# The output product of a hybrid decoder block as seven block products, with x loaded into the collecting tile

## The chip, the cores and the metric

The kernel runs on one core of a Trainium2 chip. The metric is device time in microseconds. A core has TensorE (PE, with its weight loads shown as PEld), VectorE (DVE), ScalarE (ACT), GpSimd (POOL) and SyncE (SP); each works through its own instructions in a fixed order. SP, ACT and POOL also issue DMAs, each through a queue of its own; DMAs that add into their target are issued by POOL in this kernel. On PE the clock that was granted is given in the profile as a share of full speed.

## The reference

One layer of a decoder trunk on 512 tokens with a width of 1024, all in float32. Three mixers (sparse attention, block-sparse attention, a state-space scan) are projected to the width, gated and added; the sum goes through W_out, and then comes a feed-forward block of width 4096:

```python
mix = (gates[:, :, 0] * (y_a @ w_br_dsa[l]) + gates[:, :, 1] * (y_b @ w_br_nsa[l])
       + gates[:, :, 2] * (y_c @ w_br_ssd[l]))
x = x + mix @ w_out[l]
h = rms_norm(x, norm2_g[l])
x = x + jnp.square(jax.nn.relu(h @ w_ff1[l])) @ w_ff2[l]
```

The change concerns the line with `w_out` and the norm behind it.

## The kernel before, in words

**Products.** Both operands of a large product are split into a high part (rounded by a copy to fp32r) and a low part (the rest). `mm3` issues three matmuls into the same accumulator: high × high (L454), low × high (L455), high × low (L456). All work is in this form, so a weight block costs a copy on ACT (`whi`, L173) and a subtraction on DVE or POOL (`wlo`, L175).

**The weight stream.** A class `WS` holds all weight blocks of 128 x 1024 in their order of use. `load` starts the DMA of a block on SP into one of three raw buffers (`wraw`, RAWB = 3); `split` makes the high and low parts (six pairs); a raw buffer is free again when its low part is made. `tick` keeps the splits up to three blocks ahead of use and the loads up to three ahead of the splits.

**The end of the mixers.** The generator `branches` goes through six branches; the last, b2, adds the last 256 tokens of the block-sparse mixer to `mix` (128 partitions x 8 blocks of channels x 512 tokens, held transposed). Its matmuls are 256 columns wide. For every block of channels the finished sum is split into `mixh` and `mixl` with the factor 0.5 (L1608, L1609). Then W_out follows in two halves of 512 columns: for each of four blocks of 128 tokens 8 x 3 matmuls (192 in all, 128x512). DVE adds x from its own tile `xin` (L1631) into the collecting tile `x2`; ACT squares with a sum (L1633); two small steps on DVE (L1635, L1636) and a power on POOL (L1637) give the factor of the norm; DVE writes the normed tokens `xn` (L1641); PE transposes them in eight 128x128 steps (L1647); ACT and DVE split them into `h2h` and `h2l` (L1649, L1650). x and the gain g2b come over ACT's queue, W_out's blocks over SP's.

**The feed-forward block.** `F q m` names block m of the first FF product in quarter q. The first four blocks of quarter 0 are done in two token halves of 256, so that the first half needs token blocks 0 and 1 alone. The second FF product is already done with seven block products instead of eight, quarter by quarter: `quad_block` makes the weight sums, three of them in place in the two tiles qd0 and qd1 by accumulating DMAs on POOL's queue (L275), one (t3) by an accumulating DMA onto a raw tile (L260); `left` makes the quarters of the left operand and splits them (L1727, L1728); `ff_down` issues 24 matmuls per product and adds the result to `x2` and a spare accumulator `U2`. In the last quarter these sums are made by POOL (`sums`, `less`, L1691).

**What sets the order.** The program text is written by generators that take turns (`yield` gives the length of a piece); a scheduler then sets each engine's order by its own model of the times, with priorities (`high_priority`) that pull pieces forward. The order does not change at run time.

## Time and profile before

| | us |
|---|---|
| median of three timed runs (1345.57 to 1347.51) | 1347.01 |
| the profiled execution | 1348.56 |
| its span, first to last instruction | 1346.8 |
| first matmul of W_out, from the span's start | 962.87 |
| first matmul of the feed-forward block | 1010.04 |

The mean granted clock of TensorE is 0.997. Times of instructions below are counted from the start of the span. A row of a timeline gives start, duration, engine, line, operation, result and operands, and in square brackets how long the engine had stood idle and what ended it. In a row of grouped lines the last parts are busy time and mean ns. "L1631" is line 1631 of the kernel before.

### The profile page before, as it was taken

The numbers are of one execution on the slowest core, as the hardware profiler recorded it, in microseconds if no ns is written. First come the engines' busy times: TensorE is split into PE (matmuls) and PEld (weight loads), VectorE is DVE, ScalarE is ACT, GpSimd is POOL, SyncE is SP. The second block draws the span as 40 slices with busy tenths as digits, with TensorE's granted clock in tenths as the row PEclk, the third lists the DMA queues.
The fourth block names the chain that finished last, engine by engine and source line by source line (L and its number), as shares of the span: only waits on it lengthen the run. The fifth ranks groups of instructions, "written<-read, shape, count | busy, mean of one in ns | idle before, by whom it ended". The sixth has DMA issues, their size and how long they took to land.

```text
span 1346.8 us, 19610 instructions
## 1 busy us (share of the span) xinstructions
PE 1325.0 (98%) x6803; PEld 1102.9 (82%) x6803; DVE 1011.8 (75%) x1994; ACT 739.4 (55%) x1408; POOL 301.3 (22%) x258
## 2 busy tenths in 40 slices
PE   9999999999999998999999999999999999999998
PEld 7888888888877876888888888778889888888886
DVE  6499986989967656576687889979655566667767
ACT  5455335687767766366676566655333443444452
POOL 2225111111016666600000022224000100201154
PEclk9999999999999999999999999999999999999999
DMA  6436665454579899644354546335526474756554
GB/s 200 122 91 169 186 180 135 133 153 131 145 232 326 268 290 295 183 145 118 105 155 132 156 130 181 110 98 166 187 64 188 117 179 125 172 151 156 162 110 125
DMA packets 253953, 217.94 MB, mean 162 GB/s; under 512 B 16009, under 2 KB 203293, under 8 KB 253854
## 3 DMA queue, kind: packets, MB, share of 16 engines
q1 hardware_dynamic: 209916, 164.76, 41.0%
q0 software_dynamic: 17408, 25.17, 10.1%
q10 hardware_dynamic: 26530, 26.75, 6.0%
q8 instruction: 54, 0.88, 0.3%
q14 instruction: 45, 0.37, 0.1%
...
## 4 chain that ended last, share of the span: by engine, by line
PE 80%; DMA 6%; DVE 5%; POOL 4%; issue 3%; ACT 1%; SPq 0%; POOLq 0%; ACTq 0%; DVEq 0%
PE pj L454 19%; PE pj L456 18%; PE pj L455 18%; PE sc L454 3%; PE sc L455 3%; PE sc L456 3%; PE pT L983 3%; PE pv L996 2%; PE pv L995 2%; PE sc L924 2%; PE sc L923 2%; DMA wraw<-in_w_in_dram 1%; DMA xs<-x_d 1%; DVE wlo L175 1%; DMA xz<-xzt_d 1%
## 5 line engine op out<-in xcount | busy, mean ns | idle before, releaser
L173 ACT ACTIVATE whi<-wraw 128x1024 fp32r<-128x1024 f32 (+2 forms) x188 | 196.3, 1047 | 235.6 <-PE pj L455 130.5
L175 DVE TENSOR_TENSOR wlo<-wraw,whi 128x1024 fp32r<-128x1024 f32 (+1 forms) x176 | 221.4, 1261 | 105.5 <-ACT whi L173 102.6
L454 PE MATMUL pj<-hTh,whi 128*128 128x512 f32 x512 | 204.3, 399 | 2.2 <-DVE cacc L851 2.2
L456 PE MATMUL pj<-hTh,wlo 128*128 128x512 f32 x512 | 203.0, 397 | 0.0
L455 PE MATMUL pj<-hTl,whi 128*128 128x512 f32 x512 | 202.9, 396 | 0.0
L932 ACT ACTIVATE p<-p,nb,rs 128x384 f32<-128x384 f32 (+3 forms) x160 | 107.8, 677 | 25.9 <-DVE nb L930 25.8
L454 PEld LDWEIGHTS pj<-hTh,whi 128*128 128x128 f32 x512 | 96.6, 189 | 21.3 <-ACT eab L1340 2.2
L456 PEld LDWEIGHTS pj<-hTh,wlo 128*128 128x128 f32 x512 | 96.7, 189 | 19.7 <-issue 0.8
L455 PEld LDWEIGHTS pj<-hTl,whi 128*128 128x128 f32 x512 | 96.7, 189 | 18.7 <-issue 0.6
L455 PE MATMUL pj<-h2l,whi 128*128 128x512 f32 (+1 forms) x256 | 96.3, 376 | 0.0
L456 PE MATMUL pj<-h2h,wlo 128*128 128x512 f32 (+1 forms) x256 | 96.2, 376 | 0.0
L454 PE MATMUL pj<-h2h,whi 128*128 128x512 f32 (+1 forms) x256 | 96.1, 376 | 0.0
L1042 POOL DMA_DIRECT2D qu<-q_d x32 | 23.6, 738 | 269.5 <-PE sc L924 102.3
L454 PE MATMUL pj<-whi,hTh 128*128 128x512 f32 (+2 forms) x208 | 80.5, 387 | 0.4 <-DVE cacc L851 0.4
L456 PE MATMUL pj<-whi,hTl 128*128 128x512 f32 (+2 forms) x208 | 80.3, 386 | 0.1
L455 PE MATMUL pj<-wlo,hTh 128*128 128x512 f32 (+2 forms) x208 | 79.4, 382 | 0.0
L456 PE MATMUL sc<-whi,fo 128*128 128x512 f32 x200 | 77.7, 390 | 1.7 <-DVE fo L1728 1.7
L454 PE MATMUL sc<-whi,fh 128*128 128x512 f32 x200 | 77.8, 389 | 0.0
L455 PE MATMUL sc<-wlo,fh 128*128 128x512 f32 x200 | 77.8, 389 | 0.0
L987 ACT ACTIVATE pth<-pT 128x512 fp32r<-128x512 f32 x92 | 53.0, 594 | 31.6 <-PE pT L983 31.0
L1606 POOL TENSOR_TENSOR mixf<-mixf,gld 128x512 f32<-128x512 f32 x22 | 39.4, 1796 | 118.8 <-DVE gld L1605 97.7
L988 DVE TENSOR_TENSOR ptl<-pT,pth 128x512 fp32r<-128x512 f32 x92 | 61.6, 679 | 4.7 <-ACT pth L987 4.6
...
## 6 DMA issues: line engine op xcount, KB each, us to landing
wraw<-in_w_in_dram SPq DMA_DIRECT2D x84, 512.0 KB, 4.1
wraw<-in_w_ff_dram SPq DMA_DIRECT2D x56, 512.0 KB, 4.2
qd<-in_w_ff_dram POOLq DMA_DIRECT2D x24, 512.0 KB, 5.9
...
E<-ac_d SPq DMA_DIRECT2D x16, 512.0 KB, 5.8
xz<-xzt_d SPq DMA_DIRECT2D x16, 512.0 KB, 4.8
wraw<-in_w_br_ssd_dram SPq DMA_DIRECT2D x16, 512.0 KB, 4.5
```

Of the source, the lines that this page charges most:

```text
L173: act.activation(hi[:, :m], r[:, :m], AF.Copy)
L175: (pool if i in LOWP else dve).tensor_tensor(lo[:, :m], r[:, :m], f(hi[:, :m]), op=ALU.subtract)
L454: pe.matmul(o, lh, rh, start=first, stop=False)
L455: pe.matmul(o, lh, rl, start=False, stop=False)
L456: pe.matmul(o, ll, rh, start=False, stop=last)
L923: pe.matmul(s_[:, h % w, :n], u.q[h], kh[:, :n], start=True, stop=False)
L924: pe.matmul(s_[:, h % w, :n], u.q[h], kl[:, :n], start=False, stop=True)
L932: act.activation(u.p[h][:, :n], u.p[h][:, :n], AF.Exp, bias=u.nb[:, h:h + 1], scale=rs8[:, u.b, u.h0 + h:u.h0 + h + 1], accum_out=u.sm[:, ...
L983: pe.transpose(pt[:, h], u.p[h][:, kb * 128:kb * 128 + 128], ident)
L987: act.activation(ph, ptf, AF.Copy)
L988: dve.tensor_tensor(pl, ptf, f(ph), op=ALU.subtract)
L1606: (dve if br in ("b1", "b2") else pool).tensor_tensor(mx, mx, th, op=ALU.add)
```

## The change

W_out is taken out of the stream as eight blocks of two column halves, and put in as a further "quarter" q = -1 of the seven-product scheme, in the order P0, P6, P1, P2, P4, P3, P5 (the numbers are those of `PROD`; 24 matmuls each). The left operand is quartered from `mix` itself, with the difference tiles made by POOL and DVE; the high parts are copies on ACT (L1524), the low parts DVE's, and POOL's for P0 and P6 (L1525). The factor 0.5 moves into the evacuations: L1569 on DVE, or L1557 and L1565 on ACT followed by an add on POOL (L1561, L1566). x is loaded straight into `x2` at the start of b2. W_out's quarters 11 go to qd0 and qd1, which exist only from the moment when the attention's pool is closed and b2's begins; the sums follow by accumulating DMAs (now L280, and L265 onto a raw tile). The norm's small steps are all on POOL (L1763 to L1765). Tokens 0 to 255 are finished with P4, tokens 256 to 511 with P3 and P5, so squares and norm of each half are issued there. Four low parts of weights go to POOL (`LOWW`): one of t2, and FF blocks 1 to 3.

```diff
@@ -172,7 +172,7 @@
             with tc.issue_after(HX[HB[i]][0]) if i in HB else nullcontext():
                 act.activation(hi[:, :m], r[:, :m], AF.Copy)
             with tc.issue_after(H0[0][1]) if i == 1 else nullcontext():
-                (pool if i in LOWP else dve).tensor_tensor(lo[:, :m], r[:, :m], f(hi[:, :m]), op=ALU.subtract)
+                (pool if i in LOWP or i in LOWW else dve).tensor_tensor(lo[:, :m], r[:, :m], f(hi[:, :m]), op=ALU.subtract)
...
         def tick(s):
             while s.nsplit < len(s.specs) and s.nsplit < min(s.consumed - 1 + NS, s.cur + LEAD):
+                if s.nload <= s.nsplit and s.shut():
+                    break
                 s.split()
             while s.nload < len(s.specs) and s.nload < s.nsplit + RAWB:
-                if callable(s.specs[s.nload][0]) and FL[0] is None:
+                if s.shut():
                     break
                 s.load()
+
+        def shut(s):
+            go = s.specs[s.nload][0]
+            return callable(go) and (FL[0] is None or (go.q >= 0) != FL[1])
...
-    P["wo"] = [plan_tok(A["w_out"], D, [(o * 512, 512)]) for o in range(2)]
...
-            return wcols(A["w_ff2"], D, 8 * q + 4 * row + 2 * s, 2, 512 * col, 512)
+            return wcols(A["w_out"] if q < 0 else A["w_ff2"], D, 8 * max(q, 0) + 4 * row + 2 * s, 2, 512 * col, 512)
...
                 if name == "11":
-                    t = FL[0].tile([128, 1024], F32, name=f"qd{s}", bufs=QB)
+                    t = FL[0].tile([128, 1024], F32, name=f"qd{s}", bufs=1 if q < 0 else QB)
                     nc.sync.dma_start(t.rearrange("p (a b) -> p a b", b=512), src("11"))
...
-    FL = [None]
-    FSEQ = [("F", 0, m) for m in range(8)]
+    FL = [None, False]
+    LOWW = set()
+    PLO = (0, 6)
+    FSEQ = [("G", -1, i) for i in (0, 6, 1, 2, 4, 3, 5)] + [("F", 0, m) for m in range(8)]
...
             ff[kind, q, i] = plan_ch(A["w_ff1"], 4096, q * 1024 + 128 * i)
+            if q == 0 and i in (1,2,3):
+                LOWW.add(ff[kind, q, i])
         else:
             ff[kind, q, i] = [quad_block(q, i, s) for s in range(2)]
+            if q < 0 and i in (2,):
+                LOWW.add(ff[kind, q, i][1])
...
+        ST, AO, FA, PRE = {}, {}, {}, {}
+
+        def quarters(q):
+            if q < 0:
+                return [mix[:, 4 * kh:4 * kh + 4, 256 * th:256 * th + 256] for kh, th in ((0, 0), (0, 1), (1, 0), (1, 1))]
+            return [FA[q, kh][:, th] if (q, kh) in FA else None for kh, th in ((0, 0), (0, 1), (1, 0), (1, 1))]
+
+        def less(name, a, b, eng=pool):
+            t = PRE.pop(name, None)
+            if t is None:
+                t = FL[0].tile([128, 4, 256], F32, name=name)
+            eng.tensor_tensor(t, a, b, op=ALU.subtract)
+            return t
+
+        def sums(q, part=None):
+            a11, a21, a12, a22 = quarters(q)
+            if part != 1:
+                if q < 0:
+                    ST[3] = less("fs3", a11, a21)
+                    return
+            ST[1] = less("fs", a21, a22, dve if q < 0 else pool)
+            ST[2] = less("fs2", a11, ST[1])
+            if q >= 0:
+                ST[3] = less("fs3", a11, a21)
+            ST[4] = less("fs4", a12, ST[2])
+
+        def left(n):
+            if n >= len(GSEQ):
+                return
+            q, i = GSEQ[n]
...
+            src = a11 if i == 0 else a22 if i == 5 else a12 if i == 6 else ST[i]
+            h_ = FL[0].tile([128, 4, 256], F32R, name="fh", bufs=2)
+            l_ = FL[0].tile([128, 4, 256], F32R, name="fo", bufs=2)
+            act.activation(h_, src, AF.Copy)
+            (pool if q < 0 and i in PLO else dve).tensor_tensor(l_, src, f(h_), op=ALU.subtract)
+            AO[q, i] = h_, l_
...
+        INTO = (((X11, PL), (UU, PL)), ((X22, PL), (X12, PL)), ((UU, MI),), ((X22, MI), (X21, PL)), ((X12, PL),), ((X21, PL),),
+                ((X11, PL),))
...
+        def ff_down(q, i):
+            ah, al = AO.pop((q, i))
+            pos = GSEQ.index((q, i))
+            blk = [ws.get(b) for b in ff["G", q, i]]
+            for tt in range(2):
+                p = ps(("pT", "sc", "pj")[pos and 2 - pos % 2] if q < 0 else "sc" if pos % 2 or q < 3 else "pT", [128, 512])
+                for j in range(4):
+                    wh, wl = blk[j // 2]
+                    cs = slice(128 * tt, 128 * tt + 128)
+                    mm3(p, ah[:, j, cs], al[:, j, cs], wh[:, j % 2], wl[:, j % 2], j == 0, j == 3)
+                    if tt and j % 2:
+                        ws.free(ff["G", q, i][j // 2])
+                    if tt == 0 and j == 1:
+                        left(pos + 1)
+                    yield 3 * 213
+                into = list(INTO[i])
+                if q in (-1, 0, 3) and i == 0:
+                    act.activation(UU(tt), p, AF.Copy, scale=0.5 if q < 0 else 1.0)
+                    into.pop()
+                    if q != 0:
+                        into.pop()
+                        pool.tensor_tensor(X11(tt), X11(tt), UU(tt), op=ALU.add)
+                if q in (-1, 3) and i == 1:
+                    into.pop()
+                    t1 = FL[0].tile([128, 512], F32, name="t1", bufs=2)
+                    act.activation(t1, p, AF.Copy, scale=0.5 if q < 0 else 1.0)
+                    pool.tensor_tensor(X12(tt), X12(tt), t1, op=ALU.add)
+                for d, op in into:
+                    if q < 0:
+                        dve.scalar_tensor_tensor(d(tt), p, 0.5 if op is PL else -0.5, d(tt), op0=ALU.mult, op1=ALU.add)
+                    else:
+                        dve.tensor_tensor(d(tt), d(tt), p, op=op)
+                if i == 2 and q in (-1, 2, 3):
+                    for d, op in ((X12, MI), (X21, PL), (X22, MI)):
+                        with tc.high_priority(offset=600 if q < 0 and d is X12 else 0):
+                            (dve if q == 2 or q < 0 and d is X12 else pool).tensor_tensor(d(tt), d(tt), UU(tt), op=op)
+                if q < 0:
+                    run_later()
+                    with tc.high_priority(offset=600):
+                        if i == 6:
+                            square(tt, 0)
+                        elif i == 4:
+                            square(tt, 1)
+                            norm(tt)
+                        elif i == 3:
+                            square(2 + tt, 1)
+                        elif i == 5:
+                            square(2 + tt, 0)
+                            norm(2 + tt)
...
-                mp = popen("mix", side="right")
-                mixh = mp.tile([128, KT, S], F32R, name="mixh")
-                mixl = mp.tile([128, KT, S], F32R, name="mixl")
+                fp = popen("ff", side="right")
+                wl = FL[0] = popen("wol", side="right")
+                U2 = wl.tile([128, 2, 512], F32, name="u2acc")
+                x2 = fp.tile([128, NB, D], F32, name="x2")
+                for t in range(NB):
+                    act.dma_start(x2[:, t], dram(A["x"], t * 128 * D, [[D, 128], [1, D]]))
+                left(0)
+                left(1)
+                for n in ("fs", "fs2", "fs3", "fs4"):
+                    PRE[n] = wl.tile([128, 4, 256], F32, name=n)
+                ws.tick()
...
-                if br == "b2":
-                    act.activation(mixh[:, m], mix[:, m], AF.Copy, scale=0.5)
-                    dve.scalar_tensor_tensor(mixl[:, m], mix[:, m], 0.5, f(mixh[:, m]), op0=ALU.mult, op1=ALU.subtract)
+                if br == "b2" and m in (3, 7):
+                    sums(-1, m // 7)
...
+        def square(t, o):
+            jk = n2.tile([128, 512], F32, name="jk2", bufs=1)
+            act.activation(jk, x2[:, t, o * 512:o * 512 + 512], AF.Square, accum_out=st2[:, t, o:o + 1])
+
+        def norm(t):
+            pool.tensor_tensor(st2[:, t, 2:3], st2[:, t, 0:1], st2[:, t, 1:2], op=ALU.add)
+            pool.tensor_scalar(st2[:, t, 2:3], st2[:, t, 2:3], 1.0 / D, EPS, op0=ALU.mult, op1=ALU.add)
+            pool.tensor_tensor(st2[:, t, 3:4], st2[:, t, 2:3], mhalf[:, :1], op=ALU.pow)
+            xn = n2.tile([128, D], F32, name="xn2", bufs=2)
+            for k0 in range(0, KT, 4):
+                cs = slice(k0 * 128, k0 * 128 + 512)
+                dve.scalar_tensor_tensor(xn[:, cs], x2[:, t, cs], st2[:, t, 3:4], g2b[:, cs], op0=ALU.mult, op1=ALU.mult)
+
+            def tr():
+                for k0 in range(0, KT, 4):
+                    p_ = ps("pT", [128, 4, 128])
+                    for k in range(4):
+                        pe.transpose(p_[:, k], xn[:, (k0 + k) * 128:(k0 + k + 1) * 128], ident)
+                    hsl = (slice(None), slice(k0, k0 + 4), slice(t * 128, t * 128 + 128))
+                    act.activation(h2h[hsl], p_, AF.Copy)
+                    dve.tensor_tensor(h2l[hsl], p_, f(h2h[hsl]), op=ALU.subtract)
+            defer(0, tr)
+
+        for q, i in GSEQ:
+            if q < 0:
+                yield from ff_down(q, i)
...
+        pclose("wol")
+        pclose("br")
+        pclose("gt")
         XT[0] = None
         fl = FL[0] = popen("ffl")
+        FL[1] = True
```

Three places show how the orders move. Lines of the changed kernel have other numbers: mm3 is L465 to L467, the transposes L1775, h2h and h2l L1777 and L1778, xn L1769.

POOL before, from the last add of the mixers to the FF stage (`st2` is the norm's factor, four times):

```order
L1606 TENSOR_TENSOR mixf_7601<-mixf_7601,gld_9666 128x512
L1606 TENSOR_TENSOR mixf_7601<-mixf_7601,gld_9713 128x512
L1637 TENSOR_TENSOR st2_10433<-st2_10433,mhalf_164 128x1 x4
L275 DMA qd0_10938<-in_w_ff2_dram 128x2x512
L275 DMA qd1_11027<-in_w_ff2_dram 128x2x512
```

POOL now, behind the first product (P0): `u2acc` holds P0, `fs2` to `fs4` are quarters of the left operand, `qd` and `wraw` weight sums:

```order
L1561 TENSOR_TENSOR x2_10285<-x2_10285,u2acc_10284 128x512
L1484 TENSOR_TENSOR fs3_10300<-mixf_7601 128x1024
L1561 TENSOR_TENSOR x2_10285<-x2_10285,u2acc_10284 128x512
L280 DMA qd0_10302<-in_w_out_dram 128x2x512
L280 DMA qd1_10309<-in_w_out_dram 128x2x512
L265 DMA wraw_10528<-in_w_out_dram 128x2x512
L1484 TENSOR_TENSOR fs2_10299<-mixf_7601,fs_10298 128x1024
L1484 TENSOR_TENSOR fs4_10301<-mixf_7601,fs2_10299 128x1024
L280 DMA qd0_10302<-in_w_out_dram 128x2x512
L175 TENSOR_TENSOR wlo_10524<-qd1_10309,whi_10523 128x1024
...
L280 DMA qd1_10309<-in_w_out_dram 128x2x512
L265 DMA wraw_10573<-in_w_out_dram 128x2x512
```

POOL had nothing but the four powers there; now the accumulates of "+22" (the first two of qd) stand behind adds and a difference, and those of "+21" (the second two) and of t3 among them.

DVE before, around the last three evictions of the W_out product (`x2<-pj,xin`), with the norm of token blocks 1 (`xn2_10667`) and 2 between them:

```order
L1631 TENSOR_TENSOR x2_10420<-pj_10622,xin_10428 128x512
...
L1641 SCALAR_TENSOR_TENSOR xn2_10667<-x2_10420,st2_10433,g2b_10426 128x512 x2
L1650 TENSOR_TENSOR h2l_10422<-pT_10647,h2h_10421 128x4x128
L1650 TENSOR_TENSOR h2l_10422<-pT_10654,h2h_10421 128x4x128
L1631 TENSOR_TENSOR x2_10420<-pj_10670,xin_10428 128x512
...
L1641 SCALAR_TENSOR_TENSOR xn2_10715<-x2_10420,st2_10433,g2b_10426 128x512 x2
L175 TENSOR_TENSOR wlo_10797<-wraw_10587,whi_10796 128x1024
L1650 TENSOR_TENSOR h2l_10422<-pF_10695,h2h_10421 128x4x128
...
L1631 TENSOR_TENSOR x2_10420<-pj_10718,xin_10428 128x512
```

DVE now, from t3's second block (`wlo_10623`) to the norm of token block 1 (`xn2_10687`); `wlo_10691` and `wlo_10697` are t4, the later ones FF blocks:

```order
L175 TENSOR_TENSOR wlo_10623<-wraw_10573,whi_10622 128x1024
L175 TENSOR_TENSOR wlo_10691<-qd0_10302,whi_10690 128x1024
L1569 SCALAR_TENSOR_TENSOR x2_10285<-pj_10654,x2_10285 128x512
L175 TENSOR_TENSOR wlo_10697<-qd1_10309,whi_10696 128x1024
L175 TENSOR_TENSOR wlo_10755<-wraw_10626,whi_10754 128x1024
...
L1778 TENSOR_TENSOR h2l_10423<-pF_10668,h2h_10422 128x4x128
L1778 TENSOR_TENSOR h2l_10423<-pT_10675,h2h_10422 128x4x128
L1569 SCALAR_TENSOR_TENSOR x2_10285<-pj_10766,x2_10285 128x512
L175 TENSOR_TENSOR wlo_10911<-wraw_10764,whi_10910 128x1024
L1569 SCALAR_TENSOR_TENSOR x2_10285<-pj_10788,x2_10285 128x512
L1769 SCALAR_TENSOR_TENSOR xn2_10687<-x2_10285,st2_10429,g2b_10427 128x512 x2
```

The norm of block 1 now stands behind the last eviction of the last product (`pj_10788`); before, it stood ahead of the last two evictions.

ACT now, beside these rows (`whi_10622` is t3's second block, `whi_10880` FF block 3; three more splits and squares stand where the dots are):

```order
L173 ACTIVATE whi_10622<-wraw_10573 128x1024
L173 ACTIVATE whi_10690<-qd0_10302 128x1024
L173 ACTIVATE whi_10696<-qd1_10309 128x1024
L1760 ACTIVATE jk2_10646,st2_10429<-x2_10285 128x512
L173 ACTIVATE whi_10754<-wraw_10626 128x1024
L1524 ACTIVATE fh_10709<-mixf_7601 128x1024
...
L173 ACTIVATE whi_10880<-wraw_10758 128x1024
L1777 ACTIVATE h2h_10422<-pF_10668 128x4x128
L1760 ACTIVATE jk2_10735,st2_10429<-x2_10285 128x512
L1777 ACTIVATE h2h_10422<-pT_10675 128x4x128
```

h2h of token block 0 now stands behind the split of FF block 3, whose raw buffer is the one that `wlo_10755` frees.

149 lines of the change are left out of this document (31 added, 118 removed).

## The prediction

> **What bounds the kernel now.** I read the page's first part, the table of stages, PE's waits, and then the rows around the two ends of the W_out product. The page first:
>
> ```profile
> span 1346.8 us, 19610 instructions
> PE 1325.0 (98%) x6803; PEld 1102.9 (82%) x6803; DVE 1011.8 (75%) x1994; ACT 739.4 (55%) x1408; POOL 301.3 (22%) x258
> q0 software_dynamic: 17408, 25.17, 10.1%
> ```
>
> PE is busy 98% of the span, so PE's time is the time. The third row prices the accumulating DMAs, which all go by POOL's queue: 10.1% of 16 engines' 1346.8 us is 136 us with all engines on them, for 25.17 MB, so 512 KB need 2.8 us if nothing else runs. The stages (columns: busy us of PE, PEld, DVE, ACT, POOL, then granted clock, DMA share, GB/s):
>
> ```profile
> 10.00:15.00 5.00, 4.92 (x18) 4.10 (x18) 4.55 (x9) 4.05 (x8) 0.94 (x1) 0.66 0.89 305
> 945.00:957.00 12.00, 12.00 (x101) 11.83 (x99) 7.35 (x17) 1.91 (x3) 0.00 (x0) 1.00 0.78 269
> 963.00:973.00 10.00, 10.00 (x45) 8.11 (x44) 7.83 (x14) 3.32 (x5) 0.00 (x0) 1.00 0.41 140
> 973.00:1010.00 37.00, 36.45 (x166) 29.46 (x165) 18.16 (x28) 14.23 (x25) 1.69 (x3) 1.00 0.21 58
> 1010.00:1022.00 12.00, 12.00 (x103) 11.96 (x102) 7.52 (x12) 4.00 (x7) 0.55 (x1) 1.00 0.62 174
> PE pj L454 <- DVE x L1631: 0.5, 1, 0.5
> ```
>
> The W_out product fills 963 to 1010. PE stands still there for half a microsecond, and the last row, from PE's waits over 900 to 1060, names it. DVE, ACT and DMA are at half load or less, POOL nearly idle. So the stage is pure matmul time with room on every other engine, and it stays so only while each matmul's operands are ready early. The slot of one matmul, from the chain of waits, and the two ends of the stage, from PE's timeline:
>
> ```profile
> 977.09 0.23 PE pj L454
> 977.32 0.24 PE pj L455
> 962.87 0.39 PE L454 MATMUL pj<-whi,mixh 128*128 128x512 f32 x1
> 999.24 0.40 PE L454 MATMUL pj<-whi,mixh 128*128 128x512 f32 x1
> 999.48 1.03 PE L1647 MATMUL pT<-ident,xn 128*128 128x128 f32 x8
> 1000.27 0.48 PE L455 MATMUL pj<-wlo,mixh 128*128 128x512 f32 x1
> 1010.04 0.28 PE L454 MATMUL pj<-h2h,whi 128*128 128x256 f32 x1
> ```
>
> A slot is 0.232 us (0.39 is the length of one overlapped matmul), eight transposes cost 0.8 (999.48 to 1000.27), and the first feed-forward (FF) matmul goes out at 1010.04, without a wait: the transposes of token blocks 0 and 1 were done inside the product. These two ends are what the change must beat.
>
> **What the change takes away.** 192 matmuls become 7 × 24 = 168: 24 × 0.232 = 5.6 us. The wait of 0.5 at L1631 goes, since the new accumulators rotate over more names. Together −6.1, worth that only if PE is fed as before. I name the products P0, P6, P1, P2, P4, P3, P5 in their order; their weights are 11, 21, then t1, t2, t4 made in place in the two tiles qd0 and qd1, and 22 and t3 in raw tiles.
>
> **The first weights: +0.6.** Before, W_out's first load went out at 940.33, early. Now 11 is loaded when the attention pool closes, about 947, together with x on ACT's queue:
>
> ```profile
> 940.33 0.37 SPq L154 DMA_DIRECT2D wraw<-in_w_out_dram  x1
> 947.45 2.10 ACTq L1626 DMA_DIRECT2D xin<-in_x_dram x4
> wraw<-in_w_out_dram SPq DMA_DIRECT2D x5, 512.0 KB, 3.4
> wraw<-in_w_ff_dram SPq DMA_DIRECT2D x21, 512.0 KB, 4.3
> xin<-in_x_dram ACTq DMA_DIRECT2D x4, 512.0 KB, 7.2
> DMA to landing us min/median/max: 4.7/5.9/10.0
> ```
>
> (The third to fifth rows end with the median us to landing; the last is qd's accumulates in the FF stage.) In 945 to 957 the traffic is already 269 GB/s; 1 MB more at that rate is 3.9 us. The second tile then lands near 956, and hi and lo parts take 2.3 more, while P0, which the scheduler has put among b2's matmuls, asks for it about 957. I take a wait of 0.6; ends 0 and 2.
>
> **The chain that sets the end: t3.** The engines' orders show a chain of DMAs and splits that no longer depends on how fast PE is. Its prices:
>
> ```profile
> 983.10 1.23 DVE L175 TENSOR_TENSOR wlo<-wraw,whi 128x1024 fp32r<-128x1024 f32 x1 [1.80 <-ACT whi L173]
> 991.76 0.69 DVE L1631 TENSOR_TENSOR x<-pj,xin 128x512 f32<-128x512 f32 x1 [0.94 <-PE pj L456]
> 994.40 1.41 DVE L1641 SCALAR_TENSOR_TENSOR xn<-x,st,g2b 128x512 f32<-128x512 f32 x2 [0.75 <-POOL st L1637]
> 1001.24 1.28 DVE L1650 TENSOR_TENSOR h2l<-pT,h2h 128x512 fp32r<-128x512 f32 x2
> 951.20 1.06 ACT L173 ACTIVATE whi<-wraw 128x1024 fp32r<-128x1024 f32 x1 [4.07 <-DMA g2b<-in_norm_g_dram]
> 992.55 0.63 ACT L1633 ACTIVATE jk<-x 128x512 f32<-128x512 f32 x1 [2.37 <-DVE x L1631]
> 993.09 0.19 ACT L1633 ACTIVATION_READ_ACCUMULATOR jk<-x 128x1 f32 x1
> 1010.91 0.60 ACT L1649 ACTIVATE h2h<-pT 128x512 fp32r<-128x512 f32 x1 [1.01 <-PE pT L1647]
> ```
>
> and on POOL, from the last FF group, which already works in this way:
>
> ```profile
> 1298.94 2.40 POOL L1691 TENSOR_TENSOR fs<-f,f 128x1024 f32<-128x1024 f32 x1 [0.63 <-DVE f L1685]
> 1301.42 3.39 POOL L1691 TENSOR_TENSOR fs<-f,fs 128x1024 f32<-128x1024 f32 x1
> 1308.14 1.51 POOL L1764 TENSOR_TENSOR x<-x,u2acc 128x512 f32<-128x512 f32 x1
> 1311.81 1.75 POOL L1764 TENSOR_TENSOR x<-x,u2acc 128x512 f32<-128x512 f32 x1
> L175 POOL TENSOR_TENSOR wlo<-wraw,whi 128x1024 fp32r<-128x1024 f32 x7 | 16.9, 2434 | 34.6 <-ACT whi L173 34.6
> ```
>
> Step by step:
>
> 1. P0 ends about 0.8 after 962.87, near 963.7, with b2's last work behind it. In POOL's order the two accumulates "+22" (rows L280) stand behind L1561, fs3, L1561: 1.51 + 2.40 + 1.51 = 5.4, so they start at 969.1.
> 2. The first lands 5.9 later, the second 2.8 after it: 977.8.
> 3. ACT splits that tile and then the raw tile of 22 (2 × 1.06), DVE takes the low part (1.23): 981.2. Only now is a raw buffer free.
> 4. SP loads the first half of t3's second block into it. Loads took 3.4 in the quiet stage and 4.3 in the FF stage; accumulates run beside it, so 4.3: 985.5.
> 5. POOL's accumulate onto it takes 5.9, plus 1.3 since qd1's "+21" went out about 1.5 before and needs 2.8 of the engines: it lands at L = 992.7.
> 6. DVE, in its order: that low part, t4's first, an eviction L1569 (priced as L1631), t4's second, FF block 0's. With the ACT split ahead: 1.06 + 4 × 1.23 + 0.69 = 6.7, so 999.4. This frees the raw buffer of FF block 3: loaded 4.3 later, 1003.7.
> 7. ACT splits block 3 (1.06) before it may do h2h of token block 0, a square, the other h2h (0.60 + 0.82 + 0.60); DVE then does h2l, L1569, a low part, L1569, and half of block 1's norm (0.69 + 0.69 + 1.23 + 0.69 + 0.71): 7.1, so 1010.8.
>
> Only then can PE transpose token block 1, and PE has nothing else left: P5 is over by about 1006.5, and FF needs both blocks. The first four transposes (0.4), the seam to the second four (0.2) and one h2h (0.60) put the first FF matmul at 1012.0 against 1010.04: **+2.0**. Behind it block 2's norm stands after another low part on DVE (0.71 + 1.23 + 0.71 = 2.65 after 1010.8, so 1013.5), while PE has four FF matmuls of 0.12 to fill 1012.0 onwards: about **+1.0** more. PE's own clock would have had P5 over at 962.87 + 168 × 0.232 + 0.8 + 0.6 = 1003.2, so the whole saving is given back in waits, most of them at the seam. From there on the FF orders are the same.
>
> The DMA terms carry the uncertainty. Step 2 and step 5 at the least landing of 4.7 each give 2.4 back, steps 4 and 6 at 3.4 another 1.8; one accumulate at 10.0 costs 4.1. I stay with the medians, since rows of the FF stage, which works the same way, gave them. The new POOL work before step 1 lies under b2; if POOL runs at 1.75 and 3.39, step 1 costs 1.5 more. ACT's new evacuations (L1557, L1565, 0.6 each) and the quarters' splits lie in ACT's and DVE's idle halves of 973 to 1010: nothing, or if that cover is gone 0.6 to 1.2 each in steps 3 and 6. x into the collecting tile costs nothing beyond the first weights.
>
> The sum is −6.1 + 0.6 + 8.5 in waits = **+3.0**: the profiled execution's own 1348.56 would become 1351.6, the median 1347.01 becomes **1350.0**.
>
> [...] DVE's fo, from its line, has a long case:
>
> ```profile
> L1728 DVE TENSOR_TENSOR fo<-f,fh x15: 1216/1217/2823, 1038.9 to 1334.3; 128x1024 fp32r<-128x1024 f32 x15
> ```
>
> Minimum and median are 1.22, one took 2.82, and POOL's fs above took 2.40 once and 3.39 the next time. [...]
>
> **Rivals.**
>
> *The cover holds better (same).* If the accumulates land near 4.7 and the loads near 3.4, L is 2 to 3 earlier, the first FF matmul goes out at 1009 to 1010, and block 2 still waits 1.0: −0.5 to +1, 1347 to 1348. For it: the DMA share in 973 to 1010 is 0.21. Against: those 4.7 to 10.0 come from a stage like the new one.
>
> *PE-bound after all (faster).* If L is 5 or more earlier (both accumulates at 4.7, no sharing, loads at 3.4 would be 8 earlier), DVE has nothing late when P5 ends at 1003.2. Still L1569 and half a norm follow P5's last matmul on DVE (0.69 + 0.71): transposes at 1004.7, FF at 1005.9, block 2 waits 1.0. That is −3.1: 1343.9. It needs all terms to fall on the good side.
>
> *POOL and DVE in each other's way (much slower).* This is the case on the other side of no change. Place: POOL's rows between P0 and the t3 accumulate. At 1.75 and 3.39, step 1 is 1.5 longer, and the one low part on POOL between the two "+21" accumulates (3.4 for 2.4) with the add behind it holds t3's accumulate up by 1.3 more; one landing towards 10.0 adds 2 to 4. It decides as soon as step 5's issue leaves POOL later than the load has landed. Sum +6: 1353. At the seam PE then idles over 4 us, and the stage 10 to 15 above shows the clock at 0.66 after PE stood still in the first microseconds: 0.34 × 5 = 1.7 us of matmul time lost; a like drop would make it 1354.7. [...]
>
> **How the numbers follow.** The forecast's chain 0.33, the cover that holds 0.32, PE-bound 0.20, POOL and DVE 0.15. A change under 0.2%, 2.7 us, cannot be told from none here. The forecast's own range, 1348.5 to 1352, lies a little on the near side of that bound, and the second case a little on both: faster 0.20, same 0.33, slower 0.47. The range takes in the edges of the second and third case and most of the fourth: 1343.7 to 1354.
>
> **What would show it.** Right: PE's waits list the transposes of xn (L1775) and, before them, P3's second block and P5's first matmul; the largest is 3 to 5 us between 1005 and 1012; t3's second accumulate lands between 991 and 995; the first FF matmul goes out near 1012; block 2's transposes wait about 1. Wrong: that accumulate lands before 988, or PE goes from P5 into FF with under 2 us of waits (then faster); low parts on DVE at 2 us or more, POOL's adds at 1.8 and 3.4, or a clock under 0.9 in 1005 to 1020 (then the fourth case).

## The result, and the profile after

Four runs of the changed kernel gave a median of 1366.11 us (1362.81 to 1370.78), four of the kernel before beside them 1347.26 (1345.57 to 1350.89). The ratio is 1.0137 with a 95% interval of 1.0116 to 1.0158: slower by 18.9 us, where +3.0 was forecast and 1354.0 was the upper end of the range. The direction was right, the size six times too small.

The page of the profiled execution (1362.99 us), its first part:

```profile
span 1361.3 us, 19634 instructions
PE 1328.9 (98%) x6779; PEld 1100.0 (81%) x6779; DVE 1032.5 (76%) x1994; ACT 749.5 (55%) x1417; POOL 354.7 (26%) x291
```

PE has its 24 matmuls less and is busy 3.9 us more: slower matmuls are a part of it, beside waits. The four windows that the prediction showed of before (us, then busy us of PE, PEld, DVE, ACT, POOL, granted clock, DMA share, GB/s), and two narrow ones:

```profile
945.00:957.00 12.00, 11.74 (x84) 10.73 (x83) 7.94 (x13) 6.18 (x6) 4.88 (x3) 1.00 1.04 334
963.00:973.00 10.00, 6.51 (x28) 5.41 (x28) 8.11 (x11) 1.06 (x1) 9.84 (x6) 0.74 0.59 146
973.00:1010.00 37.00, 31.71 (x129) 23.89 (x128) 34.56 (x29) 20.70 (x30) 27.26 (x18) 0.96 0.71 155
1010.00:1022.00 12.00, 8.62 (x44) 6.49 (x44) 10.02 (x15) 6.47 (x13) 7.17 (x10) 0.91 0.61 175
...
968.00:975.00 7.00, 6.36 (x16) 5.02 (x17) 3.93 (x9) 2.18 (x3) 6.76 (x5) 0.52 0.81 147
1009.00:1012.20 3.20, 3.20 (x9) 2.52 (x8) 2.68 (x6) 1.74 (x6) 3.04 (x3) 0.50 0.34 87
```

In 973 to 1010 DVE went from 18.16 to 34.56 of 37 us, POOL from 1.69 to 27.26. DVE has 29 instructions there where it had 28, but more of them are big and some are slow: 13 are 128x1024 where 5 were, and six take 1.8 to 3.4 us where the others of their shape take 0.7 to 1.2. Added up one by one the 29 take 36.9 us; at the short lengths they would take some 26.6, where the 28 of before take 19.0. The last two rows show the clock at a half, for 7 and 3.2 us, where before it was 1.00 throughout 945 to 1022.

What PE waits for between 900 and 1100:

```profile
PE pT L1775 <- DVE xn L1769: 4.8, 3, 2.3
PE sc L465 <- DVE gld L1741: 3.5, 1, 3.5
PE sc L465 <- ACT whi L173: 1.5, 1, 1.5
PE pj L465 <- ACT fh L1524: 0.6, 1, 0.6
...
PE pT L465 <- ACT whi L173: 0.3, 1, 0.3
```

With four of 0.3 to 0.5 for DVE between these it is 12.4 us together, against 0.5 before; all but 2.4 are for DVE. (The mixers' own waits of 0.2 to 0.3 us, 0.6 to 0.7 in all, are left out in both.) The longest is at the first matmul of P6, where the prediction had none. PE's timeline there, and at the seam to the feed-forward (FF) network:

```profile
968.64 0.77 PE L465 MATMUL sc<-whi,fh 128*128 128x512 f32 x1 [3.49 <-DVE gld L1741]
969.21 0.63 PE L466 MATMUL sc<-wlo,fh 128*128 128x512 f32 x1
969.63 0.63 PE L467 MATMUL sc<-whi,fo 128*128 128x512 f32 x1
...
1016.79 0.66 PE L1775 MATMUL pT<-ident,xn 128*128 128x128 f32 x4 [2.27 <-DVE xn L1769]
1018.13 0.50 PE L465 MATMUL pj<-h2h,whi 128*128 128x256 f32 x2
```

After the wait of 3.49 the matmuls start 0.43 apart, not 0.23. The first FF matmul goes out at 1018.13; before it was 1010.04.

DVE's and POOL's own rows at that first wait (the end of b2, P0 behind it) show what made DVE late:

```profile
961.87 4.56 DVE L175 TENSOR_TENSOR wlo<-qd,whi 128x1024 fp32r<-128x1024 f32 x2
...
966.79 1.04 DVE L1744 TENSOR_TENSOR mixf<-mixf,rtok 128x256 f32<-128x256 f32 x1
...
968.09 0.41 DVE L1741 SCALAR_TENSOR_TENSOR gld<-gld,sc 128x256 f32<-128x256 f32 x1
```

And POOL's:

```profile
962.03 3.31 POOL L1484 TENSOR_TENSOR fs<-mixf 128x1024 f32<-128x1024 f32 x1 [1.03 <-DVE mixf L1744]
965.31 2.24 POOL L1561 TENSOR_TENSOR x<-x,u2acc 128x512 f32<-128x512 f32 x1
967.50 2.42 POOL L280 DMA_DIRECT2D qd<-in_w_out_dram  x2
```

Two low parts, 2 × 1.23 by the rows of before, take 4.56 beside POOL's difference fs3, and fs3 takes 3.31 beside them. They stand ahead of the last gating of b2, whose result must leave PSUM before P6 may write there. With 2.1 us more for the pair and 0.6 for the mix's add behind it, nothing is left of the lead that DVE had.

Where the 18.9 us are is seen best between two marks that both kernels have: a matmul of the mixed branches (at 868.76 before, 865.73 after) and a late matmul of the first FF quarter, the 1150th from the end. Worked out from PE's records: from mark to mark 210.05 before and 223.60 after, **+13.6**; from there to the last matmul 263.20 and 267.13, **+3.9**. The second figure was not thought of at all. In the marked stretch 10.2 us ran at half clock; PE was busy in 9.4 of them, which costs some 4.7. Up to the first mark all twelve kernels of this document give PE the same instructions in the same order, and yet it comes between 864.9 and 871.0 us: so much differs ahead of the change from one execution to the next.

### The profile page after: what moved, and what is told of

The parts are those of the page before. It is cut to its first block, busy times and chain, and to the rows that moved or that the text cites. A ratio compares the mean times of both kernels' runs of the same rounds, so it can differ in the third digit from the quotient of the medians.

```text
span 1361.3 us, 19634 instructions
## 1 busy us (share of the span) xinstructions
PE 1328.9 (98%) x6779; PEld 1100.0 (81%) x6779; DVE 1032.5 (76%) x1994; ACT 749.5 (55%) x1417; POOL 354.7 (26%) x291
## 4 chain that ended last, share of the span: by engine, by line
PE 79%; DVE 8%; DMA 6%; issue 4%; POOL 2%; ACT 2%; SPq 0%; POOLq 0%; ACTq 0%; DVEq 0%
PE pj L465 18%; PE pj L467 18%; PE pj L466 17%; PE sc L466 4%; PE sc L465 4%; PE sc L467 4%; PE pT L994 3%; DVE wlo L175 2%; PE pv L1007 2%; PE pv L1006 2%; PE sc L935 2%; PE sc L934 2%; PE sc L1322 1%; DMA bcx<-bct_d 1%; DMA gld<-g_d 1%
## 5 line engine op out<-in xcount | busy, mean ns | idle before, releaser
L175 DVE TENSOR_TENSOR wlo<-wraw,whi 128x1024 fp32r<-128x1024 f32 (+1 forms) x171 | 217.1, 1273 | 109.9 <-ACT whi L173 109.6
L465 PE MATMUL pj<-hTh,whi 128*128 128x512 f32 x512 | 203.6, 398 | 2.2 <-DVE cacc L862 2.2
L467 PE MATMUL pj<-hTh,wlo 128*128 128x512 f32 x512 | 202.4, 395 | 0.0
L465 PEld LDWEIGHTS pj<-hTh,whi 128*128 128x128 f32 x512 | 96.3, 188 | 21.1 <-ACT eab L1351 2.2
L467 PEld LDWEIGHTS pj<-hTh,wlo 128*128 128x128 f32 x512 | 96.2, 188 | 19.6 <-issue 0.8
L467 PE MATMUL pj<-h2h,wlo 128*128 128x512 f32 (+1 forms) x256 | 97.7, 382 | 0.0
L465 PE MATMUL pj<-h2h,whi 128*128 128x512 f32 (+1 forms) x256 | 97.4, 381 | 0.0
L465 PE MATMUL sc<-whi,fh 128*128 128x512 f32 x216 | 85.7, 397 | 5.0 <-DVE gld L1741 3.5
L466 PE MATMUL sc<-wlo,fh 128*128 128x512 f32 x216 | 85.6, 396 | 0.3 <-DVE wlo L175 0.3
L467 PE MATMUL sc<-whi,fo 128*128 128x512 f32 x216 | 84.7, 395 | 0.2 <-DVE fo L1525 0.2
L465 PE MATMUL pj<-whi,hTh 128*128 128x512 f32 (+2 forms) x208 | 81.0, 389 | 0.6 <-ACT hTh L439 0.6
L467 PE MATMUL pj<-whi,hTl 128*128 128x512 f32 (+2 forms) x208 | 80.5, 387 | 0.0
L280 POOL DMA_DIRECT2D qd<-in_w_ff_dram x24 | 29.9, 1286 | 158.8 <-DVE wlo L175 112.6
```

The lines of the kernel that those rows point to most:

```text
L175: (pool if i in LOWP or i in LOWW else dve).tensor_tensor(lo[:, :m], r[:, :m], f(hi[:, :m]), op=ALU.subtract)
L280: pool.dma_start(QD[q, s].rearrange("p (a b) -> p a b", b=512), src(nx), accum_op=ALU.add)
L465: pe.matmul(o, lh, rh, start=first, stop=False)
L466: pe.matmul(o, lh, rl, start=False, stop=False)
L467: pe.matmul(o, ll, rh, start=False, stop=last)
```

## The experiments

Four causes were to be told apart: the chain through t3 as forecast; DVE and POOL making each other's instructions longer; DVE's sheer load; and, for the part behind the marks, the place of a tile. The stage is always the stretch between the two marks, the end what follows it, "half clock" the us of the stage at half clock; all three are from one profiled execution each, so differences of a few us in them are not to be leaned on. Products are named as in the prediction.

| kernel | median us | stage | end | half clock |
|---|---|---|---|---|
| before | 1347 to 1349 | 210.05 | 263.20 | 0 |
| after | 1366.11 | 223.60 | 267.13 | 10.2 |
| e1_pad | 1366.53 | 227.07 | 263.29 | 17.1 |
| e2_fs3 | 1371.15 (one run) | 230.84 | 266.99 | 20.5 |
| e3_dve | 1365.82 | 225.38 | 267.00 | 20.5 |
| e4_low | 1367.66 (one run) | 223.19 | 266.95 | 17.1 |
| e5_plain | 1366.07 (one run) | 223.16 | 267.12 | 17.1 |
| e6_plain_dve | 1352.37 | 213.76 | 263.24 | 10.2 |
| e7_order | 1368.79 | 230.02 | 263.35 | 17.1 |
| e8_warm | 1376.38 (one run) | 232.23 | 267.24 | 20.5 |
| e9_less | 1346.64 | 205.18 | 263.37 | 0 |
| e10_bpad | 1349.49 | 209.73 | 263.07 | 0 |

### The FF matmuls that got slower: e1_pad

In the changed kernel as it is built h2h, the normed tokens and the moving operand of the FF matmuls, starts 196,576 bytes into its partition (4064 modulo 4096) and h2l 16 KB behind it; before, they started at 103,520 and 119,904 (1120 modulo 4096). An unused tile behind h2l moves both by 896 bytes.

```
         h2l = fp.tile([128, KT, S], F32R, name="h2l")
+        h2p = fp.tile([128, 224], F32, name="h2p")
```

> The changed kernel with one unused tile of 896 bytes per partition behind h2l, so that h2h, h2l, x2 and the quarters' tiles all lie 896 bytes lower; every instruction and its order stay. In the changed kernel a feed-forward matmul on h2h or h2l takes 233 ns (227 before), and the rows of h2h start 32 bytes below a multiple of 2048. Theory 'row offset': the offset of an operand's rows in SBUF sets the slot; after the shift the slot is 227 again, the FF stage is 4.2 to 5 us shorter, W_out's products about 1 us, so the whole is 4 to 6 us faster than the changed kernel. Rival 'high region': it is the place above 196,608 bytes, where h2l and most of h2h still lie; then slots stay at 233 and the time within 1 us. Rival 'run to run': the slot has nothing to do with the kernel, and would be 227 or 233 in both.

Measured: 1366.53 (1365.25 to 1368.18), ratio 1.0131 [1.0115, 1.0148]. The FF matmuls of 1045 to 1330, grouped (behind the bar: busy us, mean ns of one overlapped matmul, idle time), first of before:

```profile
L456 PE MATMUL pj<-h2h,wlo 128*128 128x512 f32 x210 | 81.7, 389 | 0.0
```

Then of after, and under it of e1_pad:

```profile
L467 PE MATMUL pj<-h2h,wlo 128*128 128x512 f32 x224 | 88.5, 395 | 0.0
L466 PE MATMUL sc<-wlo,fh 128*128 128x512 f32 x176 | 68.7, 390 | 0.0
```
```profile
L467 PE MATMUL pj<-h2h,wlo 128*128 128x512 f32 x224 | 87.1, 389 | 0.0
```

Matmuls on h2h take 6 ns more in after; those on fh, in the same kernel and time, do not; with the tile moved the 6 ns are gone. From start to start it is 226.7 ns before, 233.0 after, 226.7 with the pad, and the end is 3.8 us shorter. That cause is shown. The rival of the high region is out: with the pad h2l and nearly all of h2h still lie above 196,608. The pad also moves W_out's left quarters fh and fo, which lay at 4064 modulo 4096 in after: from start to start W_out's matmuls go from 232 to 227 ns. The total gained nothing: the stage became 3.5 longer, with 17.1 us at half clock, although every engine's instructions stand in the same order as in after. Its waits:

```profile
PE sc L465 <- DVE gld L1741: 3.5, 1, 3.5
PE pj L467 <- DVE fo L1525: 2.6, 1, 2.6
PE sc L467 <- DVE fo L1525: 2.5, 1, 2.5
```

So the same order gives other waits from one kernel to the next: the stage is so short of DVE time that small shifts decide which instruction collides with which. That reading is argued from these rows, not shown by itself; how far the stage of one and the same kernel differs from execution to execution was not measured.

### One of POOL's instructions away: e2_fs3

```
-                    ST[3] = less("fs3", a11, a21)
+                    ST[3] = less("fs3", a11, a21, dve)
```

> The changed kernel with one difference tile (fs3) made by DVE and no longer by POOL; the scheduler then also moves some DVE instructions. Theory 'POOL and DVE block each other': two low parts on DVE that took 4.6 us beside fs3 on POOL take 2.4, PE's wait of 3.5 us for P6's accumulator goes, and so do the double slots (0.43 for 0.23) behind it: 5 to 6 us faster than the changed kernel, span 1355 to 1358. Rival 'chain of t3': the end is set by t3's accumulate, which is as late as before; the wait only moves to P3 and P5: 0 to 1.5 us faster, span 1360 to 1361.5.

One run, 1371.15, span 1369.4. The wait at P6 only fell from 3.5 to 2.8, and the blocking turned up elsewhere. DVE and POOL of this kernel around 985:

```profile
983.99 3.38 DVE L1525 TENSOR_TENSOR fo<-fs,fh 128x1024 fp32r<-128x1024 f32 x1
987.29 5.04 DVE L175 TENSOR_TENSOR wlo<-wraw,whi 128x1024 fp32r<-128x1024 f32 x1
```

POOL's:

```profile
982.95 3.33 POOL L1484 TENSOR_TENSOR fs<-mixf,fs 128x1024 f32<-128x1024 f32 x1
...
987.00 1.76 POOL L1566 TENSOR_TENSOR x<-x,t 128x512 f32<-128x512 f32 x1
...
989.24 2.00 POOL L1566 TENSOR_TENSOR x<-x,t 128x512 f32<-128x512 f32 x1
```

fo takes 3.38 beside the difference, and one low part, 1.23 by itself, takes 5.04 beside the two adds. Taking one POOL instruction away moves the collision and does not end it.

### POOL's work in the stage on DVE: e3_dve, and a part of it: e4_low

e3_dve gives DVE the differences, the adds of U2 and t1 into x2 and all low parts; POOL keeps the accumulates and the norm's small steps. The other lines left out move fs2, fs4 and the remaining adds in the same way. e4_low moves the low parts of four blocks alone (the lines with LOWW).

```
-            if q == 0 and i in (1,2,3):
-                LOWW.add(ff[kind, q, i])
...
-            if q < 0 and i in (2,):
-                LOWW.add(ff[kind, q, i][1])
...
-    PLO = (0, 6)
+    PLO = ()
...
-                    ST[3] = less("fs3", a11, a21)
+                    ST[3] = less("fs3", a11, a21, dve)
...
-                        pool.tensor_tensor(X11(tt), X11(tt), UU(tt), op=ALU.add)
+                        (dve if q < 0 else pool).tensor_tensor(X11(tt), X11(tt), UU(tt), op=ALU.add)
...
```

> The changed kernel with all tensor work of the W_out stage on DVE (the low parts of P0 and P6 and of four weight blocks, fs3, fs2, fs4, the adds of U2 and t1 into x2); POOL keeps the accumulating DMAs and the norm's small steps. Theory 'block each other': no 128x1024 instruction of DVE takes over 1.4 us, no 128x512 one over 0.8, the clock stays at 1.00 in the stage, PE's waits there fall from 12 to 4 or 5 us: about 9 us faster than the changed kernel, 1353 to 1356, and still 3 to 5 us behind the kernel before because of the 227 to 233 ns slots. Rival 'DVE full': DVE has some 17 us more to do in the stage; it becomes the bound and PE waits as long as now, 1360 or more.

> The changed kernel with the four low parts of weights (one of t2, FF blocks 1 to 3) back on DVE; POOL keeps the rest. Theory 'block each other': the norm of block 0 takes 1.4 us again instead of 3.5, the waits around P5 and at the seam (2.0, 0.5, 0.4, 2.3) fall by 2 to 3 us in all, the wait of 3.5 at P6 stays: span 1358 to 1360. Rival 'DVE full': four more low parts of 1.23 stand ahead of the norms on DVE, no gain or 1 to 2 us worse.

Measured for e3_dve: 1365.82 (1364.88 to 1368.81), ratio 1.0123 [1.0106, 1.0140]; for e4_low one run, 1367.66. DVE's groups in 945 to 1022, first of before:

```profile
L175 DVE TENSOR_TENSOR wlo<-wraw,whi 128x1024 fp32r<-128x1024 f32 x12 | 14.5, 1218 | 5.3 <-ACT whi L173 5.3
```

Of after, and under it of e3_dve:

```profile
L175 DVE TENSOR_TENSOR wlo<-wraw,whi 128x1024 fp32r<-128x1024 f32 x9 | 14.1, 1578 | 2.6 <-ACT whi L173 2.6
L1575 DVE TENSOR_TENSOR x<-x,u2acc 128x512 f32<-128x512 f32 x2 | 5.0, 2476 | 0.1
L1569 DVE SCALAR_TENSOR_TENSOR x<-pj,x 128x512 f32<-128x512 f32 x6 | 4.1, 682 | 0.5 <-PE pj L467 0.5
```
```profile
L175 DVE TENSOR_TENSOR wlo<-wraw,whi 128x1024 fp32r<-128x1024 f32 x12 | 14.6, 1219 | 1.8 <-ACT whi L173 1.7
L1571 DVE TENSOR_TENSOR x<-x,u2acc 128x512 f32<-128x512 f32 x6 | 3.8, 684 | 0.0
```

With POOL out of the way every form is back at its length: a low part at 1219 ns (1578 in after), an add of two SBUF operands at 684 (2476). The eviction, of the same size but with one operand in PSUM, took 682 in after beside the same POOL work. So the blocking is shown: in after it met the low parts and the add, and not the eviction. The wait at P6 falls from 3.5 to 0.9. But the stage is no shorter (225.38). In its place stands one large wait, on ACT; PE's waits, and ACT's timeline ahead of it:

```profile
PE pj L461 <- ACT fh L1520: 7.3, 1, 7.3
PE pT L1771 <- DVE xn L1765: 2.7, 1, 2.7
```
```profile
979.76 1.06 ACT L173 ACTIVATE whi<-qd 128x1024 fp32r<-128x1024 f32 x1 [3.72 <-DMA qd<-in_w_out_dram]
...
981.67 1.04 ACT L1520 ACTIVATE fh<-fs 128x1024 fp32r<-128x1024 f32 x1
```

P1's left operand (fh) is queued on ACT behind the split of t2, and this one waits for the accumulate that makes t2. With DVE and POOL repaired the chain of accumulates is the bound. In e4_low, nearer to the change, the low parts are gone from POOL, but its adds still collide (one add of L1571 took 5.60 on DVE), and the stage is 223.19, as in after.

### The sums of weights left out: e5_plain

The blocks of t1 to t4 are plain loads of one quarter of W_out each; the sums of quarters are left out, so this kernel computes something else, with the same matmuls, splits and evictions.

```
+        if q < 0:
+            return ws.add([(src({"t1": "12", "t2": "22", "t3": "12", "t4": "21"}.get(name, name)), 512)], 2, 512)
```

> The changed kernel with the sums of W_out's quarters left out: each product gets one quarter of W_out by a plain load on SP into a raw buffer (the output is not the layer's), so no accumulating DMA stands in the stage and the loads can run ahead. Quarters, adds and low parts stay on POOL as they are, h2h stays where it is. Theory 'chain of accumulates': most of PE's waits in the stage and the half clock behind them come from late sums; without them the span falls by 8 or more, to 1353 or less. Theory 'POOL and DVE block each other': DVE instructions of 2 to 5 us stay, and with them waits of 2 to 3.5 us at P6, at low parts of the left operand and at the norm; the span falls by 2 to 5, to 1356 to 1360.

One run, 1366.07; stage 223.16, within half a microsecond of after. The chain on which the whole forecast was built is gone here, and nothing is gained; both expectations had it faster. DVE is busy 36.36 of 37 us, and PE's largest wait is 4.3, for a left operand's low part on DVE:

```profile
973.00:1010.00 37.00, 30.65 (x122) 23.63 (x121) 36.36 (x29) 19.61 (x29) 26.11 (x17) 0.91 0.47 142
```

### Both away: e6_plain_dve

e5's loads with e3's move from POOL to DVE, and e1's pad. Sums of weights are left out here too.

> As the run without sums, and beside it all tensor work of the stage on DVE (as in the run with everything on DVE) and the 896 unused bytes behind h2l. Neither accumulates nor POOL beside DVE, and slots of 227 ns: if these three are the causes, no wait over 1.5 us but the one at the seam, the clock 1.00 throughout, and the saving of 5.6 comes through but for 2 to 3 at the seam: 2 to 4 us faster than before, 1343 to 1347 where before has 1347 to 1349. Rival 'DVE full': with 17 us more on DVE the products wait for low parts and sums all the same: 1352 or more.

Measured: 1352.37 over ten runs (1348.92 to 1356.45), ratio 1.0031 [1.0016, 1.0046]; stage 213.76, +3.7 against before (the profiled execution is the fastest of the ten).

| stage against before | weights summed by DMA | plain loads |
|---|---|---|
| POOL does its share | +13.6 | +13.1 |
| DVE does it | +15.3 | +3.7 |

Only the last of the four has e1's pad, worth some 1.8 in the stage by the slots. The medians go the same way: against before beside them +18.9, +17.6 (one run), +16.7 and +3.9. Either cause alone holds the stage at +13 to +15; that is why neither experiment alone moved it. What keeps the last 3.7 (24 matmuls less and the pad's 227 ns would make it some −6.4) shows in the window:

```profile
973.00:1010.00 37.00, 32.07 (x141) 25.59 (x140) 37.00 (x48) 22.66 (x37) 7.86 (x12) 0.90 0.54 162
```

DVE is busy all of the 37 us, with every instruction at its short length. That suggests DVE's load as what was left; e9_less tries it.

### DVE given air: e9_less

e6, and the four difference quarters and the six adds of U2 left out as well: the products take the plain quarters. Ten DVE instructions and the dependences on them go.

```
-            src = a11 if i == 0 else a22 if i == 5 else a12 if i == 6 else ST[i]
+            src = a11 if i == 0 else a22 if i == 5 else a12 if i == 6 else (a22 if q < 0 else ST[i])
...
-                if i == 2 and q in (-1, 2, 3):
+                if i == 2 and q in (2, 3):
```

> The run without sums and with everything on DVE, and now the four difference quarters and the six adds of U2 into x2 left out as well (the output is not the layer's in these points either): some 8.5 us less on DVE. In that run DVE was busy 37.0 of 37 us from 973 to 1010. Theory 'DVE full': that was what still cost it the saving; now DVE has air, PE's waits in the products go, and the kernel is 3 to 5 us faster than the one before (ratio 0.996 to 0.998). Rival 'the seam': the norm behind the last product holds PE whatever DVE has to do; the time stays within 1 us of that run (ratio 1.002 to 1.004).

Measured: 1346.64 over six runs (1344.37 to 1349.21), ratio 0.9979 [0.9964, 0.9993]; stage 205.18, 4.9 shorter than before, no half clock. The same window, and PE's largest wait:

```profile
973.00:1010.00 37.00, 34.11 (x174) 28.52 (x173) 34.48 (x43) 23.98 (x38) 8.24 (x12) 1.00 0.61 181
```
```profile
PE pj L464 <- DVE h2l L1773: 1.3, 1, 1.3
```

Some 0.9 of the 4.9 is the pad's, since W_out's matmuls take 227 ns here and 232 before; e10_bpad, the kernel before with a like pad, has 209.73. In the median 2.8 us are gained, 0.9 to 4.9 by the interval. So most of what the matmuls are worth comes back when DVE has less to do. Since the differences also feed left operands, the run takes away a dependence with the load and doesn't part the two. DVE is busy 34.48 of 37 even so, as in after: it is not the busy share by itself that tells whether PE waits.

### Other order, and a warm clock: e7_order, e8_warm

e7_order (with e1's pad) does P3 right after P1, so that t3 and its accumulate are used before t2 and t4:

```
-    FSEQ = [("G", -1, i) for i in (0, 6, 1, 2, 4, 3, 5)] + ...
+    FSEQ = [("G", -1, i) for i in (0, 6, 1, 3, 2, 4, 5)] + ...
```

> The changed kernel with the 896 unused bytes and another order of products, P0, P6, P1, P3, P2, P4, P5 (the order of the feed-forward quarters); the square of the second column half of tokens 256 to 511 moves behind P2. Each in-place sum has one more product (5.6 us) between the product that frees its tile and the one that needs it. Theory 'chain of accumulates': the waits for weights go, 5 to 8 us faster than the run with the unused bytes alone (1366.5), so 1358 to 1361. Theory 'POOL and DVE block each other': the waits only change places, 1364 or more.

Measured: 1368.79 (1366.78 to 1370.10), ratio 1.0152 [1.0124, 1.0180], stage 230.02. Waits on fo shrink from 5.1 (e1_pad) to 4.2, in three, and the norm of token block 0 takes it all:

```profile
PE pF L1776 <- DVE xn L1770: 10.4, 1, 10.4
```

This wait is not one for DVE's load. P4, which finishes these tokens, comes one product later in this order. ACT's squares wait 3.7 us for POOL's adds of U2, and a low part on DVE 3.1 us for a split behind them on ACT: in 1016 to 1026 POOL is busy 8.9 us of 10, DVE 5.8.

e8_warm fills PE's wait ahead of P6 with 28 transposes of the identity, to keep the clock up:

```
+            if q < 0 and i == 6:
+                with tc.issue_after(...LASTB[0]):
+                    for k in range(28):
+                        pe.transpose(pd[:, k % 4], ident, ident)
```

> The changed kernel with 28 transposes of the identity on PE, into a tile that nobody reads, between b2's last matmul and P6's first, where PE waits 3.5 us; the scheduler shifts some instructions of the products behind. They take about 28 x 0.11 = 3.1 us, so the wait is filled, not shortened. Theory 'the clock follows PE's idle time': no half clock behind it, so P6's twelve or thirteen matmuls of 0.43 us are 0.23 again; the first half-clock stretch of the stage (6.8 us long, 3.4 lost) is gone, and P6 ends about 3 us earlier after its first matmul. Rival 'the clock falls for another reason' (load, DMA): the stretch stays.

One run, 1376.38. P6 does run at full clock: its matmuls start 0.23 apart from 974.59 on, and the clock over 963 to 973 is 1.00, where after has 0.74 with its half clock from 967.8 on. The half clock comes later, in 973 to 1010 (0.88):

```profile
963.00:973.00 10.00, 10.00 (x79) 9.64 (x78) 9.96 (x12) 3.23 (x4) 8.92 (x4) 1.00 0.78 228
973.00:1010.00 37.00, 29.82 (x113) 22.25 (x112) 32.13 (x27) 17.08 (x21) 26.65 (x17) 0.88 0.71 148
```

The time comes no sooner: PE has other waits, the longest of 3.8 us for an h2h on ACT, and 20.5 us of the stage are at half clock. In these two runs neither PE's order nor a warm clock at one place shortened the stage. That the stage even grew by 8.6 can't be put down to one thing, since the other engines' orders shifted as well.

### The tile's place in the kernel before: e10_bpad

There mixh and mixl, the left operand of the W_out product and the stationary one of its matmuls, lie at 4064 modulo 4096. An unused tile of 896 bytes moves them to 3168.

```
                 mixl = mp.tile([128, KT, S], F32R, name="mixl")
+                mixp = mp.tile([128, 224], F32, name="mixp")
```

> The kernel before with one unused tile of 896 bytes behind mixl, so that mixh and mixl lie 896 bytes lower; nothing else changes. In it they are W_out's weight operand and start 32 bytes below a multiple of 2048, and their matmuls have slots of 232 ns. Theory 'row offset' for this operand too: 227 ns, the 192 matmuls take 1.0 us less, the whole is 0.5 to 1.5 us faster (ratio 0.9990 to 0.9996). Rival: only the moving operand's rows matter; slots stay at 232 and the time the same.

The groups of the product in 963 to 1009, of before and of e10_bpad:

```profile
L456 PE MATMUL pj<-whi,mixl 128*128 128x512 f32 x62 | 24.2, 396 | 0.0
```
```profile
L456 PE MATMUL pj<-whi,mixl 128*128 128x512 f32 x60 | 23.1, 391 | 0.0
```

From start to start 232.3 becomes 227.4 ns, and the product, first to last matmul, 46.04 us for 46.94. The total is 1349.49 against 1349.40, ratio 0.9995 [0.9982, 1.0008]: 0.9 us is less than this tells from nothing. So the slot of 0.232 on which the prediction costed the 24 matmuls was itself a slow one; at 0.227 they are worth 5.4, not 5.6. In after, whose left quarters lie at 4064 too, W_out's matmuls still take 232 ns.

## Why the prediction was wrong, and what in it was right

**The saving: right, but never reached.** 24 matmuls went; e9_less, which leaves out sums and differences, has most of them, 4.9 us of stage (0.9 of it the pad's) and 2.8 in the median.

**The chain through t3: right in its links, short in its times.** The chain of waits of after holds the links of steps 3 to 7, among them the rows below from 987.47 on; the first row is a link that the prediction did not have, the low part ahead of P6.

```profile
963.01 3.42 DVE wlo L175
...
987.47 9.62 DMA wraw<-in_w_out_dram
997.11 1.06 ACT whi L173
...
1002.22 1.21 DVE wlo L175
1003.43 3.42 DVE xn L1769 x2
```

The accumulate of t3's second block went out at 987.47, where step 5 had 985.5, and landed 9.62 later, at 997.1; step 5 had 7.2 for it and L = 992.7. The transposes of token block 1 were forecast for 1010.8 and came at 1016.79, the first FF matmul for 1012.0 and came at 1018.13; block 2's waits, about 1.0 forecast, were 0.47 and 0.55, together as forecast. But e5_plain, which has no such chain, is as slow: the chain was one of two causes that hide each other, and the forecast had only this one.

**The step that failed: DVE as an idle engine.** The prediction put new evacuations and the quarters' splits "in ACT's and DVE's idle halves of 973 to 1010: nothing". DVE's half was 18.16 of 37; its new work was never added up. e6_plain_dve measures it: 37.00 of 37, at short lengths and without blocking. In the changed kernel, with a part of the work on POOL, it was 34.56: by the sums of the single instructions given with the windows above, 7.6 us are new work there and 10.3 are longer instructions. By the windows of before and e6, in 973 to 1010 alone DVE gets some 19 us more (21.4 by the totals of the two pages) for 24 matmuls less: near 0.8 us of DVE for each matmul of 0.23. And "at half load or less" did not hold for all of the rows under it: in 963 to 973, where P6 came to wait, DVE was busy 7.83 of 10 before the change.

**The row that was overruled.** The prediction showed the long cases of fo (2.82) and fs (3.39) and still priced steps 1, 3 and 6 at the short lengths, 1.51 and 2.40 on POOL and 1.23 on DVE. Those lengths came from stages in which POOL has little to do (1.69 us in the 37 of W_out, 61 in the 301 of the FF stage before); in the new stage POOL is busy for 27 of 37 us, and a pair of low parts took 4.56 for 2.46, the two halves of a norm 3.42 for 1.41, an add 2.48 for 0.68. The eviction, with one operand in PSUM, stayed at 682 ns. The third rival, with a chance of 0.15, was this case, and its price of +6 was too small against +13.6 in the stage, since it counted the blocked links of one chain and not the load.

**A wait that nobody had: P6.** 3.5 us at 968.6, from low parts that stand ahead of b2's last gating on DVE. The prediction followed the low parts only towards the end of the stage, not what else is queued behind them at its beginning. The term for the first weights, 0.6 taken, was 0.3 (the last of the waits shown), with PE busy 11.74 of 12 us in 945 to 957: small, as forecast.

**The clock.** The third rival allowed one loss of 1.7. After shows 10.2 us at half clock, some 4.7 lost, in two places: 6.8 us from 967.8 on, inside the wait of 3.49 at P6 that ended at 968.64, and 3.4 us from 1008.8 on, behind waits of 0.42, 2.04 and 0.47. In e1_pad one wait was of 3.5 us and no other above 2.6, and there were 17.1 us of it; e9_less, with waits of 1.3, 1.2 and 0.3, stayed at full clock. So in after it also came behind waits of 2.04 and less; what wait it takes, these runs do not show. The 0.66 in 10 to 15, from which the rival took its 1.7, came when PE had been busy for all of the 8 us ahead of 10, behind a standstill of 1.9 at the very start; so that row does not show that a wait brought it.

**What was not thought of: +3.9 behind the stage.** "From there on the FF orders are the same" was right, and the matmuls still took 233.0 instead of 226.7 ns, from where a tile came to lie.

The sum, against +13.6 in the stage: waits 12.4 − 0.5 before = +11.9; half clock +4.7; slower slots of the F matmuls of 512 columns between the marks 147 × 6.3 ns = +0.9 (the 192 of 256 columns take 120 ns in both kernels); matmuls gone −5.6: +11.9, with 1.7 not assigned. A part of that lies right behind the waits, where the first matmul is often followed by the next after 0.34 us and not 0.23. To the end's +3.9 and the stage's +13.6 the two profiled executions, 14.4 apart, add −3.0 ahead of the change, which is within the 6 us by which the first mark moves among the twelve; the medians are 18.9 apart, and after's runs fall into two near 1363 and two near 1370.

**Signs named in advance.** Of "right": waits on the transposes of xn, and before them on P3's second block (1.5) and P5's first matmul (0.6), yes; the largest of 3 to 5 between 1005 and 1012, no (2.0 there, and 3.5 at P6); an accumulate landing in 991 to 995, no (997.1); FF near 1012, no; block 2's waits near 1, yes. Of the fourth case: low parts at 2 us or more, POOL's adds above 1.8 (2.24) and a difference near 3.4 (3.31), a clock under 0.9 in 1005 to 1020: yes in each case, the clock for 3.2 us of it (0.50 in 1009 to 1012.2, 0.91 over 1010 to 1022).

**Open.** Why an accumulate of 512 KB takes 6.5 to 9.7 here and 5.9 in the FF stage (medians); why after's runs differ by 7 us; how far the stage itself differs from execution to execution; how much of e9's gain is load and how much the shorter dependence. No kernel with the seven products and the right sums was faster than the kernel before.
